# Two-layer hybrid diffusion backbone on one core: all eight experts ranked on chip, routing reordered, full-row keys, grouped modulation

## Chip, cores and metric

The kernel runs on one core of a Trainium2 chip. The metric is the time of one execution on the device in microseconds (us), as the median of several runs. All weights are float32 and come from HBM in every execution.

## What is computed

Two layers run over 256 latent and 256 context tokens of width 1024. In each, a modulated norm is followed by one input projection, windowed attention with context and sink, a Fourier branch and a gated convolution, merged by gates and an output projection `w_o`. Then comes a SwiGLU block: dense in layer 0, and in layer 1 the top 2 of 8 experts, for the latent tokens alone. The parts that matter here:

```
mod = silu(c) @ w_mod[l] + b_mod[l]
sh1, sc1, ga1, sh2, sc2, ga2 = split(mod, 6)
h = rms_norm(x, g_pre_mix[l]) * (1 + sc1) + sh1
z = h @ w_in[l]
...
s_loc = einsum('bqhgd,bkhd->bhgqk', qi, ki) * scale
...
x = x + ga1 * rms_norm(merged @ w_o[l], g_post_mix[l])
h2 = rms_norm(x, g_pre_ffn[l]) * (1 + sc2) + sh2
logits = h2 @ w_router + b_router
top_val, top_idx = top_k(logits, 2)
gates = scatter of softmax(top_val) to the two experts
out = sum over e of gates[e] * ((silu(h2 @ w_gate[e]) * (h2 @ w_up[e])) @ w_down[e])
x = x + ga2 * rms_norm(out, g_post_ffn[l])
```

An expert's three matrices have 3 x 1024 x 3584 elements, 44 MB. All eight experts' weights are read, whatever the routing.

## The kernel before

**Precision.** A large product is made of three matmuls in the type fp32r: each operand is split into a high part (a cast on ScalarE, L84) and the rest (a subtraction on VectorE, L85), and TensorE adds high x high, low x high and high x low (names ending in H and L; `mm3`, L384 to L386). Small products are done in float32 from the raw tile.

**Loads.** A `Stream` (L48) holds the list of a stage's weight tiles. SP issues their loads in order, one for each free buffer; `pump` splits tiles some steps ahead of their use. A tile that is marked `whole` isn't split. The expert stream `ms` has ten buffers for tiles of 128 x 2048 (1 MB, 1.049 MB in decimal). An expert is NJ = 7 steps; each step takes two gate, two up and two down tiles, so that an expert is 42 tiles.

**Start.** Layer 0's first shift and scale are needed before any projection. `columns(k)` (L495) multiplies the weight block of 128 output channels by silu of the two conditioning vectors (stationary `sil`, two columns) with eight accumulating float32 matmuls, `row` copies the 2 x 128 result from PSUM, `turn` transposes it, `finish` adds bias and gain, `affine` applies it. For five of the eight scale blocks (`DVE_SCALES`) VectorE does the products instead (`scales`, L515).

**Scores.** `score` (L748) adds query x key-high (stationary `qq`, 128 rows: the two halves hold the query's high and low parts against the same keys, `kk`), the mask, and query x key-low (`kl`), for which only the 64 rows of the query's high part are used.

**Routing and experts.** `routing(t)` is a generator for each tile of 128 tokens: the norm behind `w_o`, the sum of squares, transposes, the router's logits. `top2` takes the two best experts, `places` ranks each token within its expert by a matmul with a triangular matrix (`rank`, L1304) and counts each expert's tokens (`cf`). Experts work on slots, not tokens: `Prep` gathers an expert's tokens into 128 slots by matmuls with a 0/1 matrix `P`, from three bf16 parts of the normalised tokens (`xparts`). Slots are fixed in advance: one position has 160 (`PX`, whose last 32 are an extra block on the raw tiles), others 128 (tiles split, slots stationary, `gemm_up`), and the `SMALL` ones 64 (class `Few`, `gemm_few`, L1720: raw float32 tiles, two column groups). `ORDER` is the order of the positions. Position 0 is expert 0, which has 128 slots whatever its count. `plan()` ranks experts 1 to 7 by count, while expert 0 is at work; `order` then reads the ranking into SP's registers, which address the weights of the later loads (`at`). Positions 1 (160), 2 to 4 (128) and 5 to 7 (64) are the experts by falling count. Expert 0's loads are issued in `mixing(1)`, behind those of `w_o` (`ms.loads()`). If an expert has more tokens than slots, a branch at the end runs a further 128-slot pass for it.

**Around an expert.** An expert's `todo` list spreads small work over its steps: gathering for the next expert (`prepare`), and scaling and scattering the one before (`combine`). Behind the last one come its scatter, the final norm and the store (`final`).

## Time and profile before

| what | us |
|---|---|
| median of three runs | 2116.42 (2114.77 to 2118.81) |
| the profiled execution, whole | 2120.59 |
| its span on the core | 2118.8 |
| TensorE busy | 2047.6 (97%) |
| VectorE busy | 1289.7 (61%) |
| ScalarE busy | 973.3 (46%) |
| DMA moved | 517.47 MB, mean 244 GB/s |

The span is what the rows count from: 0 is the start of the first instruction. PE is TensorE's matmuls and PEld its weight loads, DVE is VectorE, ACT ScalarE, POOL GpSimd, SP the engine that issues loads (SPq its queue). L12 is line 12 of the kernel before. A row `bka<-wh,xeH 128*128 128x512` is a matmul of a 128-row, 128-column stationary with a moving operand of 512 columns, from the tiles `wh` and `xeH` into the PSUM tile `bka`. The idle time in brackets is that of the engine just before, with what ended it. The granted clock is given as a share of full speed.

### The profile page before, as it was taken

The numbers are of one execution on the slowest core, as the hardware profiler recorded it, in microseconds if no ns is written. First come the engines' busy times: TensorE is split into PE (matmuls) and PEld (weight loads), VectorE is DVE, ScalarE is ACT, GpSimd is POOL, SyncE is SP. The second block draws the span as 40 slices with busy tenths as digits, with TensorE's granted clock in tenths as the row PEclk, the third lists the DMA queues.
The fourth block names the chain that finished last, engine by engine and source line by source line (L and its number), as shares of the span: only waits on it lengthen the run. The fifth ranks groups of instructions, "written<-read, shape, count | busy, mean of one in ns | idle before, by whom it ended". The sixth has DMA issues, their size and how long they took to land.

```text
span 2118.8 us, 29464 instructions
## 1 busy us (share of the span) xinstructions
PE 2047.6 (97%) x11729; PEld 1573.7 (74%) x11729; DVE 1289.7 (61%) x1624; ACT 973.3 (46%) x1255; POOL 28.5 (1%) x35
## 2 busy tenths in 40 slices
PE   8999999999999999899997999999999999999897
PEld 6766888888888888778986775566655788865685
DVE  6655766646876555775556971266422889850686
ACT  5544433244323224665446662254422677741575
POOL 0000000000000000100000000000000000000000
PEclk9999999999999999999998999999999999999999
DMA  7212354533665653233566899976799999999992
GB/s 260 98 59 75 114 159 149 159 110 102 217 198 199 211 166 119 96 117 120 174 223 253 351 344 417 420 293 246 259 399 420 420 373 363 346 371 421 420 421 107
DMA packets 93922, 517.47 MB, mean 244 GB/s; under 512 B 10480, under 2 KB 10736, under 8 KB 50768
## 3 DMA queue, kind: packets, MB, share of 16 engines
q1 hardware_dynamic: 92144, 510.39, 64.9%
q0 software_dynamic: 768, 2.49, 0.3%
q10 hardware_dynamic: 864, 2.62, 0.3%
q8 instruction: 94, 1.54, 0.3%
q14 instruction: 52, 0.43, 0.1%
HBM read 513.36 MB, written 2.10 MB: 243 GB/s over the span
## 4 chain that ended last, share of the span: by engine, by line
PE 64%; DVE 4%; ACT 4%; DMA 3%; issue 1%; POOL 0%; DVEq 0%; ACTq 0%
PE bka L1707 6%; PE bka L1709 6%; PE bka L1708 6%; PE bka L1720 5%; PE bka L386 5%; PE bka L385 5%; PE bka L384 5%; PE bkd L1776 3%; PE bkd L1778 3%; PE bkd L1777 3%; DMA raw<-in_weg 3%; PE bkd L1733 2%; DVE wl L85 2%; ACT wh L84 2%; PE bkd L384 1%; PE bka L1588 1%
## 5 line engine op out<-in xcount | busy, mean ns | idle before, releaser
L85 DVE TENSOR_TENSOR wl<-raw,wh 128x1024 fp32r<-128x1024 f32 (+1 forms) x406 | 715.1, 1772 | 247.3 <-ACT wh L84 245.3
L84 ACT CAST wh<-raw 128x1024 fp32r<-128x1024 f32 (+1 forms) x406 | 601.9, 1488 | 336.9 <-DMA raw<-in_wfg 78.9
L384 PE MATMUL bka<-hH,wh 128*128 128x512 f32 (+1 forms) x832 | 300.1, 361 | 0.7 <-ACT wh L84 0.7
L385 PE MATMUL bka<-hL,wh 128*128 128x512 f32 (+1 forms) x832 | 294.1, 353 | 1.5 <-DVE hL L351 1.5
L386 PE MATMUL bka<-hH,wl 128*128 128x512 f32 (+1 forms) x832 | 293.7, 353 | 1.7 <-DVE wl L85 1.7
L1707 PE MATMUL bka<-wh,xeH 128*128 128x512 f32 x560 | 229.9, 410 | 9.3 <-ACT wh L84 7.4
L1709 PE MATMUL bka<-wl,xeH 128*128 128x512 f32 x560 | 224.9, 402 | 6.4 <-DVE wl L85 6.4
L1708 PE MATMUL bka<-wh,xeL 128*128 128x512 f32 x560 | 223.9, 400 | 0.0
L385 PEld LDWEIGHTS bka<-hL,wh 128*128 128x128 f32 x832 | 157.2, 189 | 27.1 <-issue 2.6
L384 PEld LDWEIGHTS bka<-hH,wh 128*128 128x128 f32 x832 | 157.2, 189 | 25.5 <-issue 2.4
L386 PEld LDWEIGHTS bka<-hH,wl 128*128 128x128 f32 x832 | 157.2, 189 | 24.3 <-DVE wl L85 2.8
L246 DVE SCALAR_TENSOR_TENSOR junk<-raw,silr 128x1024 f32<-128x1024 f32 x128 | 156.3, 1221 | 5.2 <-DMA raw<-in_wmodc 3.2
L1720 PE MATMUL bka<-raw,xe 128*64 128x256 f32 x1344 | 154.1, 382 | 0.2 <-DMA raw<-in_weu 0.2
L1707 PEld LDWEIGHTS bka<-wh,xeH 128*128 128x128 f32 x560 | 107.4, 192 | 46.2 <-issue 11.5
L1720 PEld LDWEIGHTS bka<-raw,xe 128*64 128x64 f32 x1344 | 93.4, 137 | 56.4 <-issue 13.0
L1709 PEld LDWEIGHTS bka<-wl,xeH 128*128 128x128 f32 x560 | 107.3, 192 | 34.3 <-DVE wl L85 9.4
L1708 PEld LDWEIGHTS bka<-wh,xeL 128*128 128x128 f32 x560 | 107.4, 192 | 23.1 <-DVE xeL L306 0.4
L384 PE MATMUL bkd<-hH,wh 128*128 128x256 f32 (+1 forms) x320 | 114.7, 358 | 0.0
L1778 PE MATMUL bkd<-wl,htH 128*128 128x512 f32 x280 | 111.1, 397 | 2.7 <-DVE wl L85 2.7
L1776 PE MATMUL bkd<-wh,htH 128*128 128x512 f32 x280 | 112.9, 403 | 0.7 <-ACT htH L305 0.7
L1777 PE MATMUL bkd<-wh,htL 128*128 128x512 f32 x280 | 110.8, 396 | 0.2 <-DVE htL L306 0.2
L1817 DVE TENSOR_TENSOR xf<-xf,bka 128x512 f32<-128x512 f32 (+1 forms) x56 | 32.6, 583 | 121.9 <-ACT xf L1815 103.4
(373 smaller groups left out, 2848.3 us busy)
## 6 DMA issues: line engine op xcount, KB each, us to landing
raw<-in_weg SPq DMA_DIRECT2D x112, 1024.0 KB, 7.9
raw<-in_weu SPq DMA_DIRECT2D x112, 1024.0 KB, 8.8
raw<-in_wed SPq DMA_DIRECT2D x112, 1024.0 KB, 8.1
raw<-in_win SPq DMA_DIRECT2D x92, 512.0 KB, 3.4
raw<-in_wmodc SPq DMA_DIRECT2D x80, 512.0 KB, 4.2
raw<-in_wfg SPq DMA_DIRECT2D x22, 512.0 KB, 3.4
raw<-in_wfu SPq DMA_DIRECT2D x22, 512.0 KB, 4.5
raw<-in_wfd SPq DMA_DIRECT2D x22, 512.0 KB, 4.3
```

The source lines that it names most:

```text
L84: self.nc.scalar.copy(h, t)
L85: self.nc.vector.tensor_sub(l, t, h)
L384: nc.tensor.matmul(p, lhsT=lh, rhs=rh, start=first, stop=False)
L385: nc.tensor.matmul(p, lhsT=lh, rhs=rl, start=False, stop=False)
L386: nc.tensor.matmul(p, lhsT=ll, rhs=rh, start=False, stop=last)
L1707: nc.tensor.matmul(p, lhsT=q.xH[:, k], rhs=wh[:, k4], start=(k == 0), stop=False)
L1708: nc.tensor.matmul(p, lhsT=q.xL[:, k], rhs=wh[:, k4], start=False, stop=False)
L1709: nc.tensor.matmul(p, lhsT=q.xH[:, k], rhs=wl[:, k4], start=False, stop=(k == KD - 1))
L1720: nc.tensor.matmul(p[SCAP * g:SCAP * g + SCAP, i * 256:(i + 1) * 256], lhsT=q.x[:, k], rhs=w[:, k4, g * 256:(g + 1) * 256], start=(k == 0) ...
L1776: nc.tensor.matmul(py[c], lhsT=hH_[:, kk], rhs=wh[:, k2, sl], start=fst, stop=False)
L1777: nc.tensor.matmul(py[c], lhsT=hL_[:, kk], rhs=wh[:, k2, sl], start=False, stop=False)
L1778: nc.tensor.matmul(py[c], lhsT=hH_[:, kk], rhs=wl[:, k2, sl], start=False, stop=lst)
```

## The change

**Experts.** All eight experts are ranked (`Plan.choose`, seven VectorE operations on 8 x 8 tables), and `PX`, `SMALL` and `ORDER` become one position of 160, three of 128 and four of 64 slots, large and small in turns. The first expert's loads are therefore issued only when the counts are known: SP reads the first position's expert, and `ms.loads()` follows; the other seven are read later, in that expert's `todo`. Its gather, `first`, works in float32 from `X["f"]`; the three bf16 parts are made in its `todo` list. `Stream.begin` splits the first tile in two halves. The last position is a small one, whose tiles stay whole and whose tail has no splits.

**Routing of the second tile.** The first tile's steps are issued one pass of `w_o` earlier, the square is taken in two halves, and one of the two copies of the transposed tile goes to VectorE.

**Keys.** `kl` gets a copy of itself in the other 64 rows (two more subtractions of 64 x 512 for each group of keys), and the score's second matmul uses all 128 rows of `qq`.

**Modulation at the start.** All sixteen blocks go to TensorE, with the stationary padded to 32 columns (`silp`) and successive matmuls in four column groups; the four partial results are added in `turn`, by a matmul with `sel`.

The diff, cut:

```diff
-PX = 1
-SMALL = (5, 6, 7)
-ORDER = (0, 5, 1, 6, 2, 3, 7, 4)
+PX = 0
+SMALL = (4, 5, 6, 7)
+ORDER = (1, 4, 0, 5, 2, 6, 3, 7)
...
-DVE_SCALES = (0, 1, 2, 4, 6)
...
         def columns(k):
...
                 for kk in range(KD):
-                    nc.tensor.matmul(p[0:2, v * 128:(v + 1) * 128], lhsT=sil[:, kk, :], rhs=tv[:, kk], start=(kk == 0),
-                                     stop=(kk == KD - 1))
+                    g = 32 * (kk % 4)
+                    nc.tensor.matmul(p[g:g + 32, v * 128:(v + 1) * 128], lhsT=silp[:, kk], rhs=tv[:, kk],
+                                     start=(kk < 4), stop=(kk >= 4))
...
-                nc.tensor.transpose(pcol[k][:, 2 * v:2 * v + 2], rows[k][:, v * 128:(v + 1) * 128], ident[0:2, 0:2])
+                nc.tensor.matmul(pcol[k][:, 2 * v:2 * v + 2], lhsT=rows[k][:, v * 128:(v + 1) * 128], rhs=sel,
+                                 start=True, stop=True)
...
-                nc.vector.tensor_sub(kl[r], z[r], kk[r, kv])
+                nc.vector.tensor_sub(kl[r, kv], z[r], kk[r, kv])
+                nc.vector.tensor_sub(kl[halves[1 - kv], kv], z[r], kk[r, kv])
...
-                nc.tensor.matmul(c, lhsT=qq[rows, kv, j, tk], rhs=kl[rows, keys], start=False, stop=True)
+                nc.tensor.matmul(c, lhsT=qq[:, kv, j, tk], rhs=kl[:, kv, keys], start=False, stop=True)
...
                 wo_mm(pt[0][u // 4], wc[-1], u % 4, 0)
-            ms.loads()
...
             for u in range(2, 8):
-                if u == 7:
+                if u == 6:
                     run(route[0])
                     top2(0)
                 wo_mm(pt[1][u // 4], wc[u - 2], u % 4, 1)
-                if u < 6:
+                if u < 5:
                     next(route[0])
-                if u == 3:
+                if u == 4:
                     next(route[1])
-                if u == 5:
+                    next(route[0])
                     normal(0)
...
+        def choose(self):
+            one = iota[:, :NE]
...
+            nc.vector.scalar_tensor_tensor(key, cf, 8.0, one, op0=OP.mult, op1=OP.subtract)
+            nc.vector.tensor_tensor(t, inner(key), outer(key), op=OP.is_ge)
+            nc.vector.reduce_sum(out=key, in_=t, axis=AX.X)
             nc.vector.tensor_tensor(perm, inner(key), outer(one), op=OP.is_equal)
+            nc.vector.tensor_mul(t, perm, inner(one))
+            nc.vector.reduce_sum(out=key, in_=t, axis=AX.X)
+            nc.vector.tensor_scalar(cnt[:, NE + 1:], key, -1.0, None, op0=OP.add)
...
-    q = Prep(0, 0)
-    ms.pump(1)
+    pl = Plan()
+    q = Prep(ORDER[0], 0)
     next(route1)
     places(0)
-    q.pick((0,))
+    warm(3)
     next(route1)
+    normal(1)
     run(route1)
-    for c in range(2):
-        q.gather(c, ALL[:3], "a")
+    warm(8)
     wes.close()
-    normal(1)
...
-    low = ms.begin()
     top2(1)
     places(1)
-    q.pick((1,))
-    normal_low(1)
-    low()
-    for i in range(3):
-        for c in range(2):
-            q.gather(c, ((1, i),))
-    for c in range(2):
-        q.affine(c, True)
-    experts(ms, list(ORDER), 0, q, extra=True, todo=[gates, q.back] + plan())
+    pl.choose()
+    pl.units(ORDER[:1])
+    ms.loads()
+    pl.swap(rank)
+    warm(10)
+    q.first()
+    q.affine(0, True)
+    low = ms.begin()
+    cut = q.affine(1, True, False)
+    low(0)
+    cut()
+    low(1)
+    later = normal_parts(0)[:1] + normal_parts(1)[:1] + normal_parts(0)[1:] + normal_parts(1)[1:]
+    experts(ms, list(ORDER), 0, q, extra=True,
+            todo=[gates, lambda: pl.swap(gate), gate_parts, q.pick, q.back, pl.counts,
+                  lambda: pl.units(ORDER[1:], True)] + later)
```

**How the instructions move.** SP's issues behind the loads of `w_o` (`in_wo`), before: the first expert's gate and up tiles (`in_weg`, `in_weu`) follow at once.

```order
219 L76 DMA raw<-in_wco 128x1024
220 L76 DMA raw<-in_win 128x1024 x3
221 L76 DMA raw<-in_wo 128x1024 x8
222 L76 DMA raw<-in_weg 128x2048 x2
223 L76 DMA raw<-in_weu 128x2048 x2
224 L76 DMA raw<-in_weg 128x2048 x2
225 L76 DMA raw<-in_weu 128x2048 x2
```

Now a register load from the ranking (`cnt`) stands between them, and each expert load has its own address computation (`ISA`).

```order
219 L75 DMA raw<-in_wco 128x1024
220 L75 DMA raw<-in_win 128x1024 x3
221 L75 DMA raw<-in_wo 128x1024 x8
222 L1459 TENSOR_LOAD cnt
223 L1459 ISA x2
224 L75 ISA
225 L75 DMA raw<-in_weg 128x2048
226 L75 ISA
227 L75 DMA raw<-in_weg 128x2048
```

The loads of the first expert moved behind SP's read of `cnt`.

VectorE from the second tile's ranks (`rank`, in PSUM `bkt`) to the first expert's first split tile (`wl`), before:

```order
885 L1291 TENSOR_TENSOR maskh<-e_9099,e_9100 128x8
886 L1292 CAST mask<-maskh 128x8
887 L1304 SCALAR_TENSOR_TENSOR rank<-bkt,mask 128x8
888 L1478 TENSOR_SCALAR P_9368<-iota,rank 128x128
889 L1275 TENSOR_TENSOR xparts<-xf,xparts 128x1024
890 L97 TENSOR_TENSOR wl<-raw,wh 128x2048
891 L306 TENSOR_TENSOR xeL<-xf,xeH 128x512
892 L1499 TENSOR_SCALAR xf<-bka,modc_116 128x128 x4
```

and now:

```order
883 L1301 CAST mask<-maskh 128x8
884 L1313 COPY cf<-bkt 128x8
885 L1314 SCALAR_TENSOR_TENSOR rank<-bkt,mask 128x8
886 L1431 SCALAR_TENSOR_TENSOR pkey<-cf,iota 128x8
887 L1432 TENSOR_TENSOR xf<-pkey 128x64
888 L1433 TENSOR_REDUCE pkey<-xf 128x8
889 L1434 TENSOR_TENSOR xf<-pkey,iota 128x64
890 L1435 TENSOR_TENSOR xf<-xf,iota 128x64
891 L1436 TENSOR_REDUCE pkey<-xf 128x8
892 L1437 TENSOR_SCALAR cnt<-pkey 128x8
893 L1443 TENSOR_TENSOR xf<-xf,rank 128x128
894 L1444 TENSOR_REDUCE rank<-xf 128x16
```

Between the mask and the choice of slots (`P`, now in `xf`, L1504 right behind these rows) the copy of the counts (`cf`), the seven operations of the ranking up to `cnt`, and the ranks' reordering (L1443, L1444) have come in; the part `xparts` is no longer made here.

TensorE at the start, the last column blocks (`w`) up to the first projection (`hH`, `wh`), before:

```order
19 L501 MATMUL bka<-w_279,sil 2x128 x8
20 L513 MATMUL bkd<-ident,row 128x2 x2
21 L501 MATMUL bka<-w_322,sil 2x128 x8
22 L501 MATMUL bka<-w_324,sil 2x128 x8
23 L513 MATMUL bkd<-ident,row 128x2 x3
24 L384 MATMUL bka<-hH,wh 128x512
```

and now:

```order
23 L506 MATMUL bka<-w_306,silp 32x128 x8
24 L506 MATMUL bka<-w_308,silp 32x128 x8
25 L518 MATMUL bkd<-sel,row 128x2 x2
26 L506 MATMUL bka<-w_348,silp 32x128 x8
27 L506 MATMUL bka<-w_350,silp 32x128 x8
28 L518 MATMUL bkd<-sel,row 128x2 x4
29 L388 MATMUL bka<-hH,wh 128x512
```

Every block now has two groups of eight matmuls with a 32-column stationary, where five had one group with two columns, and the turn multiplies by `sel`.

## Rows read from the trace of the kernel before

**Rows 1.** Busy time by expert: us, engine busy us (instructions), granted clock, DMA share, GB/s

```profile
1142.00:1264.00 122.00, 119.68 (x560) 95.01 (x560) 102.47 (x96) 82.97 (x61) 0.00 (x0) 0.98 0.87 329
1627.00:1756.00 129.00, 127.40 (x583) 99.24 (x583) 105.92 (x65) 89.53 (x68) 0.00 (x0) 0.97 0.99 395
1756.00:1880.00 124.00, 124.00 (x595) 100.46 (x593) 105.57 (x66) 84.75 (x57) 0.00 (x0) 1.00 0.95 357
1880.00:1970.00 90.00, 85.77 (x645) 47.74 (x644) 14.11 (x21) 16.87 (x30) 0.00 (x0) 1.00 0.99 408
1970.00:2095.00 125.00, 123.32 (x529) 95.85 (x530) 103.65 (x59) 86.98 (x59) 0.00 (x0) 0.99 0.87 359
2095.00:2119.00 24.00, 10.16 (x39) 6.32 (x37) 12.23 (x16) 4.92 (x12) 4.19 (x3) 0.79 0.13 47
```

**Rows 2.** Timeline, end of second expert: start, us, instruction [idle before <-releaser]

```profile
1350.87 1.94 PE L1733 MATMUL bkd<-raw,hs 128*64 128x512 f32 x8 [0.46 <-DMA raw<-in_wed]
...
1355.28 0.50 PE L1707 MATMUL bka<-wh,xeH 128*128 128x512 f32 x1 [2.47 <-ACT wh L84]
```

**Rows 3.** Timeline, the start and the third expert: two-column blocks, first projection, 32-column block

```profile
31.84 3.66 PE L501 MATMUL bka<-w,sil 128*2 128x128 f32 x32
...
41.94 0.50 PE L384 MATMUL bka<-hH,wh 128*128 128x512 f32 x1
...
1361.68 1.08 PE L1588 MATMUL bka<-raw,xf 128*32 128x128 f32 x32
```

**Rows 4.** Timeline from the end of wo to the first expert

```profile
1118.69 2.33 PE L1312 MATMUL bka<-onesb 128*128 128x512 bf16 x10
...
1124.03 0.15 DVE L1237 TENSOR_TENSOR s<-ss 128x1 f32<-128x1 f32 x1
...
1136.27 0.17 DVE L1304 SCALAR_TENSOR_TENSOR rank<-bkt,mask 128x8 f32<-128x8 f32 x1
...
1141.75 0.79 PE L1707 MATMUL bka<-wh,xeH 128*128 128x512 f32 x1 [1.82 <-ACT xeH L305]
```

**Rows 5.** Timeline, the last expert's last down matmuls and the first of the scatter

```profile
2096.61 0.50 PE L1776 MATMUL bkd<-wh,htH 128*128 128x512 f32 x1 [0.67 <-ACT htH L305]
...
2102.80 0.40 PE L1691 MATMUL bkt<-yH,PT 128*128 128x512 f32 x1
```

**Rows 6.** DMA issues: out<-in, queue, operation xcount, KB, us to landing

```profile
raw<-xd SPq DMA_DIRECT2D x1, 1024.0 KB, 5.0
```

**Rows 7.** Timeline of a score in layer 0; busy time of a stretch of layer 1

```profile
105.10 0.39 PE L757 MATMUL bka<-kk,qq 128*128 128x512 f32 x1
105.33 0.23 PE L759 MATMUL bka<-maskb,identb 128*128 128x128 bf16 x1
105.49 0.50 PE L761 MATMUL bka<-kl,qq 64*128 64x512 f32 x1
105.92 0.50 PE L384 MATMUL bkd<-hH,wh 128*128 128x512 f32 x1
106.25 0.39 PE L385 MATMUL bkd<-hL,wh 128*128 128x512 f32 x1
...
920.00:940.00 20.00, 20.00 (x136) 16.17 (x136) 16.84 (x36) 12.80 (x27) 0.00 (x0) 1.00 0.33 106
```

**Rows 8.** Timeline, the last tile of wo

```profile
1102.76 1.04 ACT L84 CAST wh<-raw 128x1024 fp32r<-128x1024 f32 x1 [2.79 <-DMA raw<-in_wo]
...
1103.86 0.50 PE L1006 MATMUL bka<-wh,mgH 128*128 128x512 f32 x1 [1.36 <-ACT wh L84]
```

**Rows 9.** Timeline, the ranking of the experts on VectorE and the loads around SP's reads

```profile
1166.00 0.21 DVE L1424 TENSOR_TENSOR pt<-pkey 128x49 f32<-128x49 f32 x1
...
1193.98 2.53 SPq L76 DMA_DIRECT2D raw<-in_wed  x2
...
1201.22 0.81 SPq L76 DMA_DIRECT2D raw<-in_weg  x2
```

More of the change, by code (lines that the diff above doesn't have):

```diff
@@ L93, in begin, with end @@
         l = self.hl_pool.tile(self.shape, F32R, name="wl", tag="wl")
-        self.nc.scalar.copy(h, t)
-        def end():
-            self.nc.vector.tensor_sub(l, t, h)
-            self.hl.append((h, l, t))
-            self.loads()
+        n = self.shape[1] // 2
+        for c in range(2):
+            self.nc.scalar.copy(h[:, c * n:c * n + n], t[:, c * n:c * n + n])
+        def end(c):
+            self.nc.vector.tensor_sub(l[:, c * n:c * n + n], t[:, c * n:c * n + n], h[:, c * n:c * n + n])
+            if c:
+                self.hl.append((h, l, t))
+                self.loads()
         return end
@@ L204, in hybrid_kernel @@
     silb = []
+    sel = cst.tile([128, 2], F32)
+    nc.vector.reduce_sum(out=sel, in_=ident.rearrange("p (q c) -> p c q", c=32)[:, 0:2], axis=AX.X)
     for s in range(2):
@@ L558, in hybrid_kernel @@
                 turn(t - 1)
-                scales(t - 1)
             if t > 1:
@@ L752, in score @@
                 mx, nm = sm_[b, kv][:2]
-                rows = halves[kv]
                 keys = slice(k0 * 128, (k0 + nk) * 128)
@@ L1337, in experts_end @@
                 a["wed"][bass.ds(at[e], 1), j, h].rearrange("a p c -> p (a c)")
-            stream.add(src)
+            stream.add(src, whole=stream is ms and e in SMALL)
     def experts_open():
@@ L1489, in gather, with first, affine @@
                                      start=(j == 0 and i == (0, 0)), stop=(j == 3 and i == (1, 2)))
-        def affine(self, c, first=False):
+        def first(self):
+            P = f2[:, 2, :2 * CAP].rearrange("p (t s) -> p t s", s=CAP)
+            for t in range(2):
+                nc.vector.tensor_scalar(P[:, t], iota, rank[:, t, self.e:self.e + 1], None, op0=OP.is_equal)
+            for c in range(2):
+                self.bk[c] = bank("a")
+                for t in range(2):
+                    for j in range(4):
+                        k = 4 * c + j
+                        nc.tensor.matmul(self.bk[c][:, j * 128:(j + 1) * 128], lhsT=X["f"][:, t, k * 128:(k + 1) * 128],
+                                         rhs=P[:, t], start=(j == 0 and t == 0), stop=(j == 3 and t == 1))
+        def affine(self, c, first=False, cut=True):
             other = first and c == 1
@@ L1833, in experts @@
         table(AF.Sqrt)
-        low = stream.begin()
-        transposes(prev)
-        low()
+        if isinstance(pr, Few):
+            transposes(prev)
+        else:
+            low = stream.begin()
+            transposes(prev)
+            for c in range(2):
+                low(c)
         give = downs(prev, True)
```

154 lines of the change are left out of this document (77 added, 77 removed).

## Prediction

> **What bounds the kernel now.** I read the span by stages first (busy time by stretch), then the waits at the borders of the stages, then single instructions. The expert stage runs from 1142 us to the end of the span at 2118.8. In the table by expert [rows 1] the reader is to see three things. TensorE is the bound: it is busy in 119.7 of the 122 us of the first 128-slot expert and in all 124.0 of the sixth. A 128-slot expert takes 122 to 129 us, a 64-slot expert 90. And the loads run at 0.99 of the DMA engines in the 64-slot expert, 408 GB/s, so that a tile of 1.049 MB takes 2.57 us and an expert's 42 tiles 108 us: more than a 64-slot expert's time, less than a 128-slot one's. A 64-slot expert therefore eats the stock of loaded tiles (ten buffers), and the next 128-slot one refills it. Where the stock is gone shows at the border: the first large matmul after a small expert waits 2.47 us for the cast of a tile just landed [rows 2].
>
> Ahead of the experts TensorE is busy throughout, but for the two ends of the dense part: the start up to 41.94 us [rows 3] and the routing, from 1118.69 to 1141.75 us [rows 4].
>
> **The change, part by part.**
>
> *One large expert becomes a small one.* Before, expert 0 kept 128 slots unranked; now all eight are ranked, so five experts of 128 or 160 slots and three of 64 become four and four. The order was large, small, largest, small, large, large, small, large; now it is large, small, largest, small, large, small, large, small. The first five agree, so I cut both programs at 1756.0. Before: 124.0 + 90.0 + 125.0 + 23.8 to the end of the span [rows 1] = 362.8. Now: a small one behind a large one, 90; a large one behind a small one, 125 and 129 in the two that stand so [rows 1], 127 taken; a last small one, which prepares no successor but whose last tiles come at the pace of the loads, 88 taken; and the tail. In the tail 24 down matmuls from 2096.61 to 2102.80 [rows 5] become two batches of eight passes of 1.94 us each [rows 2]: 3.9 for 6.2, and the last scaling, now behind all of them, gives 0.7 back, so 22. Sum 327, a gain of **35 us**. Bounds: 28 (both added small ones run dry at their ends) and 38. Cover: the loads must have refilled the stock behind each single large expert. The fifth expert moved 395 GB/s for 129 us [rows 1], that is 48 tiles for the 42 it used, six in stock again; a small one uses 42 and is brought 35 in its 90 us, seven short. It just about closes.
>
> The Trainium skill, in DMA: Bandwidth & Descriptors, Specifications, gives one core a limit of about 358 GB/s per core from HBM. By it an estimate of 2.93 us a tile and 123 us an expert would come out, a small expert would take as long as a large one, and the exchange would bring nothing. The trace differs: 408 GB/s [rows 1], and the measurement decides.
>
> *Grouped modulation at the start.* Before, a column block of 16 two-column matmuls took 3.66 us for 32 passes, and five of the eight blocks of scales went to VectorE; the first projection matmul came at 41.94 [rows 3]. Now every block has 32 passes with a stationary of 32 columns, in four column groups in turn. The same shape stands in the 160-slot expert: 32 passes in 1.08 us [rows 3]. The 16 blocks' halves come to 8 x 1.08 = 8.6 us of TensorE, VectorE loses ten 1024-wide products, and the loads become the limit: 10.7 MB ahead of the last block at 408 GB/s are 26 us, and with about 1 us to the first issue and 2.4 of latency (5.0 for a 1 MB load alone [rows 6] less 2.57) the last lands at some 29.5. A block, a row copy, the turn and the cast of the first weight tile that stands ahead on ScalarE are 3 to 4 us more: first projection near 33.5, **8 us** earlier. Bounds: 0 (the affine and split steps of VectorE and ScalarE take over) and 10.
>
> *Full-row keys.* The second score matmul used 64 rows; it starts 0.39 us after the first (the mask matmul between), its successor 0.43 after it and the next 0.33 after that [rows 7], where matmuls of this width follow each other at 0.23 (the pitch of the first to the mask row). With 128 rows I expect 0.23 and 0.23: 0.30 us a score. There are 48 scores (32 in layer 0, 16 in layer 1): 14.4 us, all on TensorE's path, which is busy in all 20 us of a stretch there [rows 7]. VectorE is busy in 16.84 of these, so a little is lost: **13 us**. Bounds: 0 and 16. The two more key subtractions per layer lie beside projections.
>
> What the rows show is that a 64-row matmul between full ones costs its neighbours time. The Trainium skill, TensorEngine Tiling (Array Packing), Key Properties, says that a change of tiling mode drains the array. By that rule the keys' gain is real, and the grouped start pays for two changes in each block, at a time when the engine waits for loads; the sum stays as it is.
>
> *The loads of wo.* Expert 0's tiles no longer stand behind wo's in SP's queue. The last wo tile's cast waited 2.79 us for its DMA and TensorE 1.36 for the cast [rows 8]; the tile before came late too. **3.5 us** gained, between 0 and 5.
>
> *Routing of the second tile.* From the end of wo to the first expert matmul it took 23.1 us [rows 4]. The sum of squares stood at 1124.03, behind the first tile's top-2 and two 1024-wide splits on VectorE; these are now earlier or later, and the subtraction that ran on GpSimd beside the top-2 is gone from there, which together frees some 5.7 us. Against that the weights are now asked for only when all counts are known: seven ranking operations at 0.21 us and a gap each, 1.7 [rows 9]; one register load on SP, 0.7 (seven lie between the loads issued up to 1196.5 and from 1201.22 on [rows 9]), and the issue, 0.4; a landing, 5.0 [rows 6]; half a cast, 1.0. These 8.8 replace the 5.5 from the rank (1136.27) to the first matmul [rows 4]; the gather runs beside the load. Net **-2.5 us**, between -6 and +6.
>
> *A dry start of the first expert.* By the code it had nine tiles asked for long before its first matmul; now the first is only just there. TensorE needs a tile each 2.9 us (122.0 / 42 [rows 1]), the loads bring one each 2.57, so it starves only while the two-stage split is behind: I take **+2**, between 0 and 8. By its end the loads are seven tiles ahead, as much as before. The four normalisation splits moved into it add some 9 us of VectorE and ScalarE work, beside 122 us of TensorE where VectorE is busy 102.
>
> Sum: -35 - 8 - 13 - 3.5 - 2.5 + 2 = **-60 us**. The profiled execution took 2120.6 (1.8 of it around its span), which gives 2060.6; the median of the runs shown is 2116.4, 0.2% lower, and the forecast is **2056 us** against it.
>
> **Rivals.**
>
> *A, the dry start costs in full.* Weights come one by one, each through cast and subtraction, and each early tile stalls; the clock is granted at half for some of it. For it: nothing is requested before the counts. Against: the pace of loads is above that of TensorE. Price: the bounds +8 and +6 in place of +2 and -2.5: 12 to 15 us, 2069.
>
> *B, the small experts run on the loads alone.* With one large expert between two small ones the stock isn't refilled; six tiles of 2.57 us missing at each of the two later small ones are 15 each at most, and if a small expert took the loads' 108 us throughout, twice 18: 2071 to 2090. For it: the stock closes within one tile. Against: the sixth expert ran at 0.95 and the last at 0.87 of the loads [rows 1], so behind a large expert the buffers had been full before its end.
>
> *C, the gains of the dense part don't come.* The 32-column groups follow each other one by one, or the vector engines set the pace of the first blocks and of the scores: -21 shrinks to near 0, 2077.
>
> *D, slower: an expert overflows its slots.* The fifth largest of the eight counts must now be at most 64; before, only the fifth largest of experts 1 to 7. From 65 tokens on, the closing branch runs a whole further large pass from a dry start: 122 us, 23 for its preparation and 24 for a second tail [rows 1, 4], 2056 + 169 = 2225. The rule decides by counts: routed through the reference on the given inputs they are 129, 96, 78, 65, 46, 40, 39 and 19. Sorted, 129 fits 160, three fit 128 and four fit 64, so only a rounding that flips many tokens would bring it.
>
> **How the numbers follow.** Forecast as summed 0.74; A 0.11; B 0.06; C 0.07; D 0.02. The range leaves out D, and of B and C their far ends: 2040 (the favourable bounds: -3 for the exchange, -2 start, -3 keys, and -7 for loads, routing and dry start together, rounded down) to 2078 (A, the near end of B, and C). A measurement of this kernel can tell 0.2%, some 4 us, from no change: all cases but D are faster by more than that, so faster 0.97; within 0.2% 0.01, for several of the bounds together; slower 0.02.
>
> **What would show it.** In the changed profile: five large and three small experts' stretches become four large and four small, the small ones of 88 to 92 us; the first projection matmul near 33.5 us; the second score matmul followed after 0.23 us; no wait for a wo load; the first expert matmul about 20 us behind wo's last; the last expert's matmuls 64-slot ones and a tail of 22 us. It is wrong if small stretches grow past 100 us, if TensorE's idle time in the first expert passes 8 us, if the first projection stays behind 38 us, or if large-expert matmuls follow the last tail.

## The result, and the profile after

The changed kernel takes 2058.02 us (median of four runs, 2056.39 to 2060.37) against 2115.6 us for the kernel before in the same comparison: a ratio of 0.9728, 95% interval 0.9711 to 0.9744. It is 57.6 us faster; 2056 had been forecast, in a range of 2040 to 2078. Its profiled execution took 2058.32 us with a span of 2056.6, 62.2 us less than the span before. The profiles differ by 4.6 us more than the medians; that part belongs to the profile before, as a second profile of that kernel showed (below).

The expert stage of the changed kernel, in the view of busy time by stretch (columns as in [rows 1]; the third and the fourth expert, 178 and 94 us as before, are left out):

```profile
1114.00:1237.00 123.00, 119.90 (x560) 95.34 (x560) 107.97 (x87) 89.04 (x67) 0.00 (x0) 0.98 0.99 404
1237.00:1328.00 91.00, 87.53 (x699) 49.22 (x697) 12.98 (x24) 19.50 (x35) 0.00 (x0) 1.00 0.98 403
...
1600.00:1728.00 128.00, 126.41 (x584) 98.14 (x586) 103.00 (x63) 82.11 (x55) 0.00 (x0) 0.97 1.00 402
1728.00:1819.00 91.00, 85.98 (x644) 47.65 (x644) 14.11 (x21) 16.88 (x30) 0.00 (x0) 1.00 0.99 405
1819.00:1946.50 127.50, 126.28 (x582) 97.95 (x582) 103.00 (x63) 82.12 (x56) 0.00 (x0) 0.97 1.00 404
1946.50:2030.00 83.50, 79.74 (x577) 43.62 (x576) 11.74 (x15) 9.99 (x17) 0.00 (x0) 1.00 0.97 400
2030.00:2056.60 26.60, 10.83 (x44) 3.30 (x42) 9.18 (x14) 5.80 (x14) 4.26 (x3) 0.77 0.45 179
```

Two things are to be seen. Each expert keeps the length that its kind had before: large ones 123 to 128 us, small ones 91. And the DMA share (the last but one column) is 0.97 to 1.00 in every row but the tail, in the large experts too (only the third, of 178 us, has 0.76), where [rows 1] still had 0.87 to 0.99. The span splits like this:

| stretch | before | after | change | forecast |
|---|---|---|---|---|
| start to first projection matmul | 41.94 | 35.42 | -6.5 | -8 |
| from there to the end of the output projection | 1076.8 | 1057.6 | -19.1 | -16.5 (keys -13, loads -3.5) |
| from there to the first expert matmul | 23.1 | 20.9 | -2.1 | -2.5 |
| first five experts | 614.3 | 613.9 | -0.3 | +2 |
| from there to the end of the span | 362.8 | 328.7 | -34.1 | -35 |

The five changes sum to -62.2. Against the second profile of the kernel before, the first two would be -4.6 and -14.4. The start, in the timeline (what answers to [rows 3]):

```profile
31.92 0.65 PE L506 MATMUL bka<-w,silp 128*32 128x128 f32 x16 [0.64 <-DMA w<-in_wmodk]
32.50 0.61 PE L518 MATMUL bkd<-sel,row 128*128 128x2 f32 x4
33.18 1.04 ACT L83 CAST wh<-raw 128x1024 fp32r<-128x1024 f32 x1 [1.94 <-DMA raw<-in_win]
34.13 0.36 ACT L512 COPY row<-bka 128x256 f32<-128x256 f32 x1
...
34.55 1.01 PE L518 MATMUL bkd<-sel,row 128*128 128x2 f32 x4 [1.44 <-ACT row L512]
...
35.42 0.77 PE L388 MATMUL bka<-hH,wh 128*128 128x512 f32 x1
```

Sixteen passes take 0.65 us, and TensorE waits for the load of the last block (the 0.64 behind `<-DMA`): the blocks are at the pace of the loads, as forecast. But the last row copy (34.13) stands behind the cast of the first projection's weights on ScalarE, which itself waited 1.94 us for its load.

A score of layer 0 (what answers to [rows 7]):

```profile
98.63 0.39 PE L754 MATMUL bka<-kk,qq 128*128 128x512 f32 x1
98.86 0.23 PE L756 MATMUL bka<-maskb,identb 128*128 128x128 bf16 x1
98.90 0.47 PE L758 MATMUL bka<-kl,qq 128*128 128x512 f32 x1
99.21 0.39 PE L388 MATMUL bkd<-hH,wh 128*128 128x512 f32 x1
99.44 0.40 PE L389 MATMUL bkd<-hL,wh 128*128 128x512 f32 x1
```

The key-low matmul starts 0.27 us after the first one, its successor 0.31 after that, the next 0.23 later: 0.81 us in all, where [rows 7] had 0.39, 0.43 and 0.33, that is 1.15.

From the end of the output projection to the first expert matmul (what answers to [rows 4, 9]):

```profile
1093.06 2.33 PE L1320 MATMUL bka<-onesb 128*128 128x512 bf16 x10
...
1094.58 0.15 DVE L1233 TENSOR_TENSOR s<-ss 128x1 f32<-128x1 f32 x1
...
1103.49 0.15 DVE L1314 SCALAR_TENSOR_TENSOR rank<-bkt,mask 128x8 f32<-128x8 f32 x1
...
1105.15 0.17 DVE L1437 TENSOR_SCALAR cnt<-pkey 128x8 int32<-128x8 f32 x1
...
1106.54 0.91 SPq L75 DMA_DIRECT2D raw<-in_weg  x2
...
1112.88 1.99 ACT L95 CAST wh<-raw 128x1024 fp32r<-128x1024 f32 x2 [2.42 <-DMA raw<-in_weg]
...
1113.98 0.79 PE L1730 MATMUL bka<-wh,xeH 128*128 128x512 f32 x1 [3.92 <-ACT wh L95]
```

The second tile's sum of squares (`s<-ss`) stands 1.5 us after the end of the output projection (5.3 in [rows 4]) and the rank 10.4 us after it (17.6); the ranking takes 1.8 from there, SP 1.2, the first load 6.3 and the half cast 1.1: 10.5 us from the rank to the first expert matmul, against 5.5 before.

### The profile page after: what moved, and what is told of

Read it like the earlier page. It is cut to its first block, busy times and chain, and to the rows that moved or that the text cites. A ratio compares the mean times of both kernels' runs of the same rounds, so it can differ in the third digit from the quotient of the medians.

```text
span 2056.6 us, 29676 instructions
## 1 busy us (share of the span) xinstructions
PE 1979.7 (96%) x11877; PEld 1505.6 (73%) x11877; DVE 1179.8 (57%) x1564; ACT 886.5 (43%) x1204; POOL 26.7 (1%) x36
## 3 DMA queue, kind: packets, MB, share of 16 engines
q8 instruction: 95, 1.56, 0.3%
## 4 chain that ended last, share of the span: by engine, by line
PE 81%; DMA 7%; DVE 5%; ACT 5%; issue 1%; SPq 0%; POOL 0%; DVEq 0%; ACTq 0%
PE bka L390 7%; PE bka L388 7%; PE bka L389 7%; PE bka L1743 6%; PE bka L1730 5%; PE bka L1732 5%; PE bka L1731 5%; PE bkd L388 4%; PE bkd L390 4%; PE bkd L389 4%; PE bkd L1756 3%; DMA raw<-in_weg 3%; DMA raw<-in_wed 3%; DVE wl L84 3%; PE bkd L1805 3%; PE bkd L1807 3%
## 5 line engine op out<-in xcount | busy, mean ns | idle before, releaser
L84 DVE TENSOR_TENSOR wl<-raw,wh 128x1024 fp32r<-128x1024 f32 (+1 forms) x365 | 621.5, 1713 | 226.9 <-ACT wh L83 226.2
L83 ACT CAST wh<-raw 128x1024 fp32r<-128x1024 f32 (+1 forms) x365 | 523.8, 1441 | 310.6 <-DMA raw<-in_wfg 77.6
L1743 PE MATMUL bka<-raw,xe 128*64 128x256 f32 x1792 | 206.3, 382 | 3.1 <-DMA raw<-in_weu 1.8
L1730 PE MATMUL bka<-wh,xeH 128*128 128x512 f32 x448 | 186.2, 416 | 11.6 <-ACT wh L83 7.7
L1732 PE MATMUL bka<-wl,xeH 128*128 128x512 f32 x448 | 181.3, 405 | 6.0 <-DVE wl L84 6.0
L1743 PEld LDWEIGHTS bka<-raw,xe 128*64 128x64 f32 x1792 | 124.3, 137 | 80.0 <-issue 16.3
L1731 PE MATMUL bka<-wh,xeL 128*128 128x512 f32 x448 | 180.4, 403 | 0.0
L1756 PE MATMUL bkd<-raw,hs 128*64 128x512 f32 x448 | 103.0, 597 | 4.9 <-DMA raw<-in_wed 4.3
L390 PE MATMUL bkd<-hH,wl 128*128 128x256 f32 (+1 forms) x320 | 105.3, 329 | 1.0 <-DVE wl L84 1.0
L389 PE MATMUL bkd<-hL,wh 128*128 128x256 f32 (+1 forms) x320 | 105.2, 329 | 0.0
```

The source lines that it names most:

```text
L83: self.nc.scalar.copy(h, t)
L84: self.nc.vector.tensor_sub(l, t, h)
L389: nc.tensor.matmul(p, lhsT=lh, rhs=rl, start=False, stop=False)
L390: nc.tensor.matmul(p, lhsT=ll, rhs=rh, start=False, stop=last)
L1730: nc.tensor.matmul(p, lhsT=q.xH[:, k], rhs=wh[:, k4], start=(k == 0), stop=False)
L1731: nc.tensor.matmul(p, lhsT=q.xL[:, k], rhs=wh[:, k4], start=False, stop=False)
```

## The experiments

Every run changes one thing against the changed kernel, unless it says otherwise. Its distance is the difference of the two ratios to the kernel before, times 2116 us; each ratio has an interval of about 0.0016 to either side, that is 3.4 us, so that a distance is uncertain by some 5 us. Where that is too coarse, the profiles' own landmarks are used. They are single profiles, and where other runs show how far a landmark moves without an edit, that is said. The last projection matmul and the last matmul of w_o are the last of those that multiply high x high.

**The keys undone.**

```diff
-        kl = kp.tile([128, 2, 512], F32R, name="kl", tag="gg")
+        kl = sp.tile([128, 512], F32R, name="kl")
...
-                nc.vector.tensor_sub(kl[r, kv], z[r], kk[r, kv])
-                nc.vector.tensor_sub(kl[halves[1 - kv], kv], z[r], kk[r, kv])
+                nc.vector.tensor_sub(kl[r], z[r], kk[r, kv])
...
+                rows = halves[kv]
...
-                nc.tensor.matmul(c, lhsT=qq[:, kv, j, tk], rhs=kl[:, kv, keys], start=False, stop=True)
+                nc.tensor.matmul(c, lhsT=qq[rows, kv, j, tk], rhs=kl[rows, keys], start=False, stop=True)
```

> The changed kernel with the keys as before: the score's second matmul on 64 rows, kl without its second copy. Theory (a 64-row matmul between full ones costs its neighbours time): the two gaps behind it return to about 0.37 and 0.34 us, the score stretches grow by 11.7 us in layer 0 and 2.3 us in layer 1, as they shrank between the two profiles, and the kernel is 13 us slower than the changed one, 10 to 16. Rival (the scores got faster because VectorE had less to do in the changed kernel's start): 0 to 3 us.

Measured: 2074.3 us, ratio 0.9799 (0.9782 to 0.9815), 15.0 us slower than the changed kernel. From the first to the last projection matmul the profile has 1045.6 us against 1030.2, 15.4 more (without an edit there, this stretch takes 1028.8 to 1031.6 in the other runs). The timeline of a score in layer 0 again shows the row at 64 rows, 0.39 us behind the first matmul:

```profile
84.39 0.39 PE L754 MATMUL bka<-kk,qq 128*128 128x512 f32 x1
84.62 0.23 PE L756 MATMUL bka<-maskb,identb 128*128 128x128 bf16 x1
84.78 0.50 PE L758 MATMUL bka<-kl,qq 64*128 64x512 f32 x1
```

Beside it only the extra subtractions went, which takes work off VectorE: the second matmul's rows are worth 15 us, 0.31 us for each of the 48 scores.

**The slots undone.**

```diff
-SMALL = (4, 5, 6, 7)
-ORDER = (1, 4, 0, 5, 2, 6, 3, 7)
+SMALL = (5, 6, 7)
+ORDER = (1, 5, 0, 6, 2, 3, 7, 4)
```

> The changed kernel, all eight experts ranked and the first loads behind the ranking, but with the slots of before: one position of 160, four of 128, three of 64, in before's order large, small, largest, small, large, large, small, large. Theory (TensorE's time in a large against a small expert, with the loads just keeping up): 34 us slower than the changed kernel, 30 to 38. Rival (the loads set the whole expert stage, so that the exchange brought little and the 34 us came from the ranking): under 12 us slower.

Measured: 2095.08 us, ratio 0.9898 (0.9881 to 0.9914), 36.0 us slower. The fifth and sixth expert, both large, take 253 us together, and the last large one's stretch and tail 150.1 (the view of busy time by stretch):

```profile
1600.00:1853.00 253.00, 251.44 (x1174) 199.69 (x1174) 211.83 (x130) 174.47 (x124) 0.00 (x0) 0.99 0.96 378
1853.00:1944.30 91.30, 86.21 (x646) 47.77 (x645) 14.14 (x22) 16.89 (x30) 0.00 (x0) 1.00 0.98 404
1944.30:2064.60 120.30, 118.72 (x505) 92.05 (x506) 99.00 (x57) 81.85 (x54) 0.00 (x0) 0.97 0.90 369
2064.60:2094.40 29.80, 15.71 (x62) 10.80 (x61) 17.07 (x20) 10.22 (x17) 4.22 (x3) 0.85 0.11 39
```

TensorE is busy in 251.4 of the 253 us: it is the time of the large expert that went, and the rival falls. What this run still gains over the kernel before, 21.6 us, is about what the keys, the start and the routing have in the other runs and the profiles (15, 3.4 to 6.5, 2.1), so that ranking all eight brings little by itself; it is what allows the fourth small expert.

**Two small experts side by side.**

```diff
-ORDER = (1, 4, 0, 5, 2, 6, 3, 7)
+ORDER = (1, 2, 4, 0, 5, 6, 3, 7)
```

> The changed kernel with another order of the same positions: large, large, small, largest, small, small, large, small, so that two small experts are neighbours. Theory (a small expert eats a stock of loaded tiles that only a large one refills): the second of the pair runs on the loads alone and takes 104 to 108 us instead of 91, the kernel is 13 us slower than the changed one, 9 to 18. Rival (TensorE alone sets each expert's time, the order is free): within 4 us of the changed kernel.

Measured: 2072.35 us, ratio 0.9796 (0.978 to 0.9812), 14.4 us slower. The pair:

```profile
1631.50:1724.06 92.56, 89.48 (x674) 48.12 (x670) 14.86 (x22) 11.52 (x21) 0.00 (x0) 1.00 0.99 398
1724.06:1831.79 107.73, 89.04 (x635) 42.61 (x635) 8.34 (x18) 12.51 (x27) 0.00 (x0) 1.00 1.01 421
```

The first takes 92.6 us, the second, with the same work, 107.7 at the loads' full rate: TensorE is idle in 18.7 us of them. The stock of loaded tiles is real, one small expert uses it up, and the turns of large and small are what hides the loads.

**The start undone.** The edit puts back the two-column stationary, the transposes and the five blocks on VectorE (the lines with - of the diff above).

> The changed kernel with the start of before: two-column stationary, five of eight blocks of scales on VectorE. Theory: the first projection matmul returns to about 41.9 us from 35.4, and as the first projections behind it waited for their weights about 1 us less before, the kernel is 5.5 us slower than the changed one, 4 to 8. Rival (the start is bound by the loads in either form): 0 to 2 us.

Measured: 2062.81 us, ratio 0.9744 (0.9728 to 0.976), 3.4 us slower, and 4.8 by the medians. The first projection matmul comes at 42.17, the last projection at 1073.2 against 1065.7. The size is as expected at the landmark; the time of the whole allows anything from -1 to 8.

**All blocks on TensorE, one column group.**

```diff
-                    g = 32 * (kk % 4)
-                    nc.tensor.matmul(p[g:g + 32, v * 128:(v + 1) * 128], lhsT=silp[:, kk], rhs=tv[:, kk],
-                                     start=(kk < 4), stop=(kk >= 4))
+                    nc.tensor.matmul(p[0:2, v * 128:(v + 1) * 128], lhsT=sil[:, kk, :], rhs=tv[:, kk], start=(kk == 0),
+                                     stop=(kk == KD - 1))
...
```

> The changed kernel with all sixteen column blocks on TensorE, but with the two-column stationary of before in one column group, and without the padded copy of it. Theory (the four column groups in turn are what pays): 32 passes take 3.66 us as before, eight pairs of blocks 29 us instead of 8.6, and the first projection matmul comes at 48 to 52 us, 13 to 16 us behind the changed kernel's 35.4. Rival (what paid is that VectorE lost its ten products, and the loads cover TensorE's passes): first projection before 39 us.

Measured: 2067.31 us (two runs), ratio 0.9756 (0.9737 to 0.9776), 5.9 us slower by the ratios and 9.3 by the medians; the first projection matmul at 46.97, 11.6 us later than in the changed kernel. The last blocks in the timeline:

```profile
38.86 3.65 PE L502 MATMUL bka<-w,sil 128*2 128x128 f32 x32
42.45 0.28 PE L514 MATMUL bkd<-ident,row 2*128 2x2 f32 x2
42.66 3.66 PE L502 MATMUL bka<-w,sil 128*2 128x128 f32 x32
46.24 0.28 PE L514 MATMUL bkd<-ident,row 2*128 2x2 f32 x2
```

TensorE is now the bound, block behind block, 5 us later than with the split of before. The expected time was 1 us too late, but the rival falls: without the groups it would have been wrong to take the products from VectorE.

**The first expert's loads early.** The first position's expert is a constant, and its loads are issued in `mixing(1)`, in short:

```diff
+        experts_units(ms, [ORDER[0]], {ORDER[0]: 6}, SMALL)
...
+            ms.loads()
...
-    pl.units(ORDER[:1])
+    at[ORDER[0]] = 6
```

> The changed kernel, but the number of the first position's expert is written in as a constant, so that its loads are issued behind those of the output projection as before, and not behind the ranking; the ranking itself stays. Theory 1 (from the first request to the end of the second expert the loads set the pace: 84 tiles of 2.57 us and a first landing of 6 us are 222 us, and the changed kernel takes 221.5 from the first request to the third expert): the first expert matmul comes 3 to 4 us earlier and the third expert starts 4 to 8 us earlier, of which up to 3 are lost at the end of the output projection, where the loads stand behind one another; in all 1 to 6 us faster. Rival A of the prediction (a dry start costs in full): 8 to 14 us faster. Rival (TensorE sets the pace from the first matmul on): 3 us faster at the first matmul and nothing behind it.

Measured: 2054.88 us, ratio 0.9703 (0.9687 to 0.972), 5.3 us faster by the ratios and 3.1 by the medians. The first expert matmul comes 19.1 us after the last matmul of w_o against 21.6, and from there the first two experts take 214.0 us in both. So in these two profiles the loads behind the ranking cost 2.5 us at the first matmul and nothing behind it. Rival A is out.

The rival on TensorE's pace gave these numbers, but theory 1, that the loads pace the first two experts, is not refuted by them: the third expert starts 4.0 us earlier, the edge of what it expected. The other runs even speak for it. With the loads behind the ranking and the routing untouched, their first expert matmul comes 20.2 to 21.7 us after the last matmul of w_o, and where it comes early, the first two experts take longer, up to 216.1 us. From the last matmul of w_o to the third expert it is 234.8 to 236.3 us with the loads behind the ranking, and 233.1 here, where they are issued 33 us earlier: 2 to 3 us in all. TensorE and the loads are nearly level there, and the run does not separate them. Nor is the output projection slower with the loads behind it: 26.0 us from the last projection matmul to the last matmul of w_o, against 26.7.

**The routing order undone.**

```diff
-                if u == 6:
+                if u == 7:
                     run(route[0])
                     top2(0)
...
-                if u < 5:
+                if u < 6:
                     next(route[0])
-                if u == 4:
+                if u == 3:
                     next(route[1])
-                    next(route[0])
+                if u == 5:
                     normal(0)
```

> The changed kernel with the first tile's routing steps issued between the passes of the output projection where they stood before (one pass later); the square in halves and the copy on VectorE stay. Theory: the way from the end of the output projection to the first expert matmul grows by 2 us, 0 to 4, from 20.9. Rival (the way is set by the second tile's own chain, which the order of the first tile's steps doesn't touch): within 0.5 us.

Measured: 2058.5 us, ratio 0.971 (0.9694 to 0.9726), not to be told from the changed kernel. From the last matmul of w_o to the first expert matmul it is 22.1 us against 21.6, but that holds the time of the first load, which moves by more than this from run to run. To the issue of that load it is 14.6 us against 14.2 (14.2 to 14.5 in the other runs). The rival holds: the order in the passes of the output projection is worth half a microsecond at most; the way is that of the second tile's own chain.

**Five small experts, one overflowing.**

```diff
-SMALL = (4, 5, 6, 7)
-ORDER = (1, 4, 0, 5, 2, 6, 3, 7)
+SMALL = (3, 4, 5, 6, 7)
+ORDER = (1, 4, 0, 5, 2, 6, 7, 3)
```

> The changed kernel with one position of 160, two of 128 and five of 64 slots, in the order large, small, largest, small, large, small, small, small: the fourth expert by count has 65 tokens, one more than its slots, so that the closing branch runs a further 128-slot pass. Theory (rival D of the prediction and its price): 36 us less for one more small expert, some 15 more for small ones side by side, 169 more for the pass, in all 148 us slower than the changed kernel, 115 to 175. Rival (the further pass hides beside the tail or its loads come early): less than 100 us.

Measured: 2214.97 us (two runs), ratio 1.0453, 153 us slower than the changed kernel, 96 slower than the kernel before. Of the three small experts side by side the second takes 104.5 us. One token beyond 64 costs a whole pass: its loads are issued at 2056, its first matmul is at 2063.3, the last up matmul starts at 2176.4 and the span ends at 2215.1. That is the price of rival D, confirmed as a price; on the given inputs the change stays clear of it.

**Less work for TensorE in the large experts.**

```diff
-                    nc.tensor.matmul(p, lhsT=q.xL[:, k], rhs=wh[:, k4], start=False, stop=False)
```

> The changed kernel without the low x high matmul in the gate and up products of the experts of 128 and 160 slots: 448 of the matmuls at 0.232 us, 104 us of TensorE's work, are left out, and the output is that of a less precise product. It asks what bounds the changed kernel's expert stage. Theory 1 (TensorE in the large experts, the loads in hand): 90 to 104 us faster than the changed kernel. Theory 2 (the loads are at their limit nearly everywhere now): all 336 tiles at 2.57 us behind a first landing at 1112.9 end at 1974 instead of 2038, so that no more than 64 us can be gained, 40 to 64.

Measured: 2008.34 us (two runs), ratio 0.9484 (0.9467 to 0.9502), 51.6 us faster for 104 us of TensorE's work. The last expert tile lands at 1988.7, 49.4 us earlier than the 2038.1 of the changed kernel. The stretches of the fifth and the sixth expert:

```profile
1567.80:1677.30 109.50, 102.87 (x470) 75.33 (x470) 101.55 (x63) 80.93 (x55) 0.00 (x0) 0.98 1.01 421
1677.30:1778.00 100.70, 88.98 (x645) 46.81 (x644) 14.10 (x21) 16.89 (x30) 0.00 (x0) 1.00 1.01 421
```

The large one now takes 109.5 us, the loads' own pace, and the small one has grown to 100.7. Theory 2 holds: the changed kernel's TensorE and its loads are almost level, and half of what was saved on TensorE there went to waiting.

**Two edits at the start and at the first expert.**

```diff
                 turn(k + 3)
+            if k == 4:
+                ws.pump(1)
...
-            if k == 3:
-                ws.pump(1)
...
+            if self.cut and self.i_dma == 0:
+                n = self.shape[1] // 2
+                for c in range(2):
+                    self.nc.sync.dma_start(out=t[:, c * n:c * n + n], in_=ap[:, c * n:c * n + n])
```

> The changed kernel with two edits that the runs so far point to. At the start the cast of the first projection's weights goes behind the last row copy on ScalarE, which it held up (the copy came 1.5 us after its matmul). And the first expert tile is loaded in two halves, each with its own cast as now, since nothing else waited at the first expert matmul (the rest of it was ready 2.8 us earlier). Theory: first projection matmul at 34.3 instead of 35.4, first expert matmul 2 us earlier behind the end of the output projection, 3 us faster in all, 1 to 4. Rival (the loads set the pace behind both places, what is gained is waited for again): within 1 us.

Measured: 2057.61 us (five runs), ratio 0.9716 (0.9703 to 0.9729): not to be told from the changed kernel. Both edits do what they should where they stand. The first projection matmul comes at 33.97 instead of 35.42 (34.6 to 35.4 in the runs without the edit), the first expert matmul 19.2 us behind the last matmul of w_o instead of 21.6 (20.2 to 21.7). Neither reaches the end: the last projection matmul is at 1065.5 against 1065.7, and the second expert starts at 1238.5 against 1237.3. What is known of the loss at the first expert stands in the section on the hardware. No version found here that ranks all experts on chip and keeps the precision beats the changed kernel by more than can be measured.

**The kernel before without early loads, and the kernel before again.** The edit on the kernel before:

```diff
                 wo_mm(pt[0][u // 4], wc[-1], u % 4, 0)
-            ms.loads()
```

> The kernel before with one edit: expert 0's first loads are not issued behind those of the output projection but some 20 us later, when it has ended. Theory of the prediction (the expert loads delay the last loads of the output projection): the time from the last projection matmul to the last matmul of w_o falls from 29.1 to 26 to 27 us; the first expert matmul follows as before, so that the kernel is 2 us faster than the one before, or the later loads eat it. Rival (the late tile was an accident of that profile, as the run with the constant expert showed 26.0 us with the loads issued early): 26 to 27 us in both this run and another profile of the kernel before.

> The kernel before, unchanged, for a second profile beside the run without early loads. Theory (the expert loads delay the output projection): 28 to 30 us from the last projection matmul to the last matmul of w_o again. Rival (an accident of the first profile): 26 to 27 us.

Measured: without early loads 2119.41 us, ratio to the kernel before 1.0005 (0.9996 to 1.0014). From the last projection matmul to the last matmul of w_o it takes 26.0 us, and in the second profile of the kernel before, with the loads early, 26.2: the rival holds. In every other profile here, of either kernel, it is 25.9 to 26.9 us; the 29.1 of the first profile stand alone, and why is not shown. The cast of the last w_o tile in that second profile waits 1.56 us, where [rows 8] had 2.79, and TensorE waits 0.16 us for it instead of 1.36:

```profile
1097.65 1.05 ACT L84 CAST wh<-raw 128x1024 fp32r<-128x1024 f32 x1 [1.56 <-DMA raw<-in_wo]
```

The second profile of the kernel before has a span of 2113.1 us, 5.7 less than the first: 2.0 at the start, 1.9 between the first and the last projection matmul and 2.9 at w_o, while the stretch from the first expert matmul on is 1.0 longer. That covers the 4.6 us by which the two profiles differ more than the medians.

## Why the prediction held, and where it did not

*One large expert becomes a small one, -35.* Right: -34.1 in the profile, 36.0 by the run with the old slots. Its parts came as 91.2, 127.6 and 109.9 for the last with its tail, where 90, 127 and 110 (88 and 22) had been put. Rival B's mechanism is real (the pair cost 14.4 us) but the order of the changed kernel stays just clear of it, as the count of the stock had said.

*Full-row keys, -13.* Right in mechanism, somewhat too small: 15.0 by the run, with 0.31 us a score where 0.30 had been read. The prediction had taken off 1.4 us for VectorE in layer 1; the sum of the run shows no such loss.

*Grouped modulation, -8.* The mechanism was right, the term too large: -6.5 at the first projection matmul in the two profiles, and 3.4 to 4.8 in the time of the run. (The old start ends at 40.0 to 42.2 us in four profiles, the new one at 34.6 to 35.4.) The step that failed is the landing of the last load. It had been put at some 29.5, and TensorE gets the last block at 31.92, with a wait for its load. The sum had the loads at 408 GB/s from about 1 us on; the changed kernel's busy time by stretch has less in the first 5 us:

```profile
0.00:5.00 5.00, 1.57 (x7) 1.58 (x8) 0.62 (x5) 2.99 (x4) 1.24 (x8) 1.00 0.58 157
5.00:31.90 26.90, 20.90 (x323) 17.38 (x321) 11.49 (x41) 17.55 (x34) 0.00 (x0) 0.94 1.02 408
```

At 157 GB/s they brought 0.8 MB, which take 1.9 us at 408, so that 3.1 us were lost where 1 had been put; behind them the rate is that of the sum. The 3 to 4 us behind the last load came out as 3.5, of which 1.6 are a row copy that stood behind a cast still waiting for its load. The run that moves the cast has 2.4 us there and reaches 33.97, near the 33.5 of the prediction but by other parts. The time does not follow, and where the gain goes is not shown: from the first to the last projection matmul that run takes 1031.6 us, the runs without the edit 1028.8 to 1031.6.

*The loads of wo, -3.5.* Wrong in its cause. What the prediction took for the effect of the expert tiles standing behind those of w_o was a wait of that one profile; two with early loads, the constant expert and the second profile of the kernel before, have the short time as well. In the medians this term is nothing. Its size agreed with the first profile, and hid that the keys brought more.

*Routing, -2.5.* Right in size (-2.1; against the kernel before, the other runs with this routing have -2.1 to -3.6). The rank came 7.2 us earlier against the end of the output projection, where 5.7 had been put, and 5.0 of that were paid back from the rank to the first expert matmul, 10.5 us for the 8.8 put: the load took 6.3 us instead of 5.0. In eight other runs with the same issues it took 4.9 to 6.4; why is not shown. The traces say where the 7.2 came from. 3.8 were gained at the sum of squares, which no longer stands behind the two splits, 1.7 from there to the second tile's logits, and 1.7 from the logits to the rank, where one step of the top-2 had taken 1.97 us beside GpSimd's subtraction (the kernel before, then the changed one):

```profile
1132.02 2.13 POOL L1273 TENSOR_TENSOR xf<-xf,xparts 128x1024 f32<-128x1024 f32 x1 [4.91 <-ACT xparts L1269]
1132.20 1.97 DVE L1286 SCALAR_TENSOR_TENSOR e<-lg,m,sm 128x8 f32<-128x8 f32 x1
...
1101.09 0.23 DVE L1295 SCALAR_TENSOR_TENSOR e<-lg,m,sm 128x8 f32<-128x8 f32 x1
```

That the subtraction caused it is argued from these rows; of the edits here only the order of the passes was undone by a run, and it is worth no more than 0.5.

*Dry start, +2.* 0.8 more in the first expert, inside the bounds. In the runs whose first load came sooner, and with it the first expert matmul, the first expert took up to 2.5 us longer than in the kernel before.

The sum of the terms as the runs have them, 36 + 15 + 3.4 to 4.8 + 2.1 - 0.8, is 56 to 57 us for the 57.6 measured; -60 had been forecast from the first profile, and what was too much in the start and in w_o (7 us) was for the most part made up by the keys, the exchange and the dry start (4 us). That the time came within 2 us of the forecast is in this part luck.

The rule that a change of tiling mode drains the array (the Trainium skill, TensorEngine Tiling (Array Packing), Key Properties) agrees with the keys' rows, although no run here shows that a drain is what takes the time: with the same tile shape throughout, the gaps around the second score matmul shrink by 0.34 us. And the limit of about 358 GB/s a core (the Trainium skill, DMA: Bandwidth & Descriptors, Specifications, where it is half of a stack's 716) does not hold for this kernel, which runs on one core: the DMA moves 400 to 405 GB/s from 1600 to 2030 us in the changed kernel and 421 where the loads alone set the pace.

## What to carry to other kernels

Where two resources take turns at being the limit, count the stock between them expert by expert: a cheaper stage is worth its full difference only while the neighbours refill what it eats, and an order of the stages is part of the price. Take a second profile before a wait of two or three microseconds is made a term of a sum. And before a partition range is cut in half to save work, look at the start of the next matmul: here half the rows cost more than all.

## What the hardware showed that was not expected

An earlier first expert matmul bought nothing. In the run with the tile in halves TensorE's clock stayed low for longer. These rows of busy time by stretch are the changed kernel's, from its first expert matmul on; the third number from the end is the granted clock:

```profile
1114.00:1122.00 8.00, 7.96 (x23) 5.90 (x24) 7.57 (x5) 6.84 (x5) 0.00 (x0) 0.66 1.01 425
1122.00:1130.00 8.00, 6.82 (x29) 4.88 (x27) 5.26 (x11) 5.56 (x7) 0.00 (x0) 1.00 1.02 424
```

The same in the kernel with the tile loaded in halves, which started 2.4 us earlier and then waited 1.39 us for the rest of the first split, and again behind it:

```profile
1111.50:1122.00 10.50, 7.84 (x17) 5.01 (x18) 7.39 (x9) 5.89 (x6) 0.00 (x0) 0.56 1.01 415
1122.00:1130.00 8.00, 8.00 (x27) 6.30 (x27) 5.19 (x12) 5.56 (x7) 0.00 (x0) 0.72 1.01 426
```

In the first 10.5 us only 17 matmuls run, at a granted clock of 0.56, near the lower of the two levels (1.2 and 2.4 GHz), and it is still 0.72 in the next 8, where the changed kernel has 1.00 and runs 29. Between them the two kernels have done 52 and 44 matmuls by 1130. In the changed kernel TensorE had idled 3.92 us ahead of its start and then ran through its first 8 us (busy 7.96); here it started sooner and was interrupted. That this is why the clock stayed low is only argued: no run holds the waits apart from the clock.

Nor is a low clock needed for the loss. In the run with the old slots, where nothing was changed at this place, the first load took 4.9 us instead of 6.3 and the first expert matmul came 1.4 us sooner behind w_o, yet the second expert started no sooner: 145.2 us behind the last matmul of w_o against 144.9. The first 24 us from the first expert matmul on, in the changed kernel and in that run:

```profile
1113.98:1137.98 24.00, 22.08 (x83) 16.76 (x84) 20.80 (x22) 18.73 (x17) 0.00 (x0) 0.89 1.01 424
1112.32:1136.32 24.00, 19.97 (x77) 14.47 (x77) 19.16 (x22) 18.13 (x15) 0.00 (x0) 0.93 1.01 422
```

There the clock is the higher one, the loads run at their full rate in both, and TensorE is busy for 2.1 us less. With the loads issued early (the constant expert) the second expert starts 142.4 us behind w_o. So the pace of the loads takes a head start away as well, and how much of it was the clock in the run with the halves stays open.

In the first profile of the kernel before a low clock stands behind a wait, too: behind the 1.36 us at w_o [rows 8] the granted clock is 0.53 for 3.6 us, ten matmuls at about half speed (busy time by stretch):

```profile
1103.00:1105.40 2.40, 1.02 (x3) 0.59 (x4) 1.57 (x2) 1.41 (x3) 0.00 (x0) 1.00 0.98 410
1105.40:1109.00 3.60, 3.60 (x10) 2.77 (x10) 1.33 (x5) 0.89 (x3) 0.00 (x0) 0.53 1.03 423
```

That wait cost itself and, behind it, as much again: ten matmuls that take 2.3 us at the pitch of 0.23 [rows 7] took 3.6. It is not so behind every wait: at the same place in the second profile TensorE waits 0.47, 0.16 and 0.53 us, and the granted clock stays at 1.00.
